# A one-core decoder step: the first weight block in two pieces, and gate products tied to the block three before

## The chip, the cores and the metric

The kernel runs on one core of a Trainium2 chip. The metric is the device time of one execution in microseconds (us), lower is better. Five engines work side by side on a core, each through its own queue in order: TensorE (PE, matrix products; PEld is its loading of weights), VectorE (DVE), ScalarE (ACT), GpSimd (POOL) and SyncE (SP, which here issues nearly all DMA transfers). They meet only at semaphores.

## The reference, cut to what matters

```python
# 512 prompt rows and 64 sample rows share the weights; D_MODEL = 1024
xn = rms_norm(x, attn_norm_g)
q, k, v, su, sv, g_a, g_b = split(xn @ w_in)             # 30 blocks of 128 columns
A  = window_attention(q, k, v)                           # window 128, 8 query heads
B  = gelu(su) * (W_s @ layer_norm(gelu(sv)))
x1 = x + (sigmoid(g_a) * (A @ w_branch_a) + sigmoid(g_b) * (B @ w_branch_b)) @ w_out
# product-key retrieval over 128 x 128 experts, 8 heads, 16 picks each
idx, gate = top16(rms_norm(x1) @ w_q, sub_keys)
x2 = x1 + sum_k gate_k * gelu(rms_norm(x1) . peer_u[idx_k]) * peer_v[idx_k]
x3 = x2 + sigmoid(rms_norm(x2) @ w_ple_gate) * (p @ w_ple)
```

All of it is in float32.

## The kernel before, in words

Every float32 matrix product is made of three products of split operands: a weight block `w_raw` is split into `w_hi` (a copy on ScalarE, line 66) and `w_lo` (what is left, a subtraction on VectorE, line 67), and so is the other operand. `load_block` allots `w_raw` (four buffers), issues its load on SyncE, and splits it with a raised priority. A scheduler sets the order of each engine's instructions when the kernel is built, from the order of the code, priorities, buffers and its own idea of durations; the order is fixed from then on.

**The start.** SyncE loads `vecs`, the first weight block (128 partitions x 8 x 128, 512 KB) and the eight tiles of the transposed input `xT[k]` (288 KB each; their buffers are called `c` or `c4` in the rows). ScalarE and VectorE split the weight block, scale and split each `xT[k]` into `xn[0][k]` and `xn[1][k]` (lines 181 and 182; tiles `x`), and sum the squares for the norm (squares line 140, sums line 142, tiles `rstd` and `t`). TensorE's first column chunk (`w_chunk(0)`, line 205) goes through k = 0 to 7 with six matmuls each (three products, two column ranges of 256 and 320), so that it can follow the input tiles as they come. Chunk 1 (tile `pv`, line 82) follows with the next weight block.

**The experts.** 384 of the rows are computed against all 16384 experts, in 128 blocks of 128. Stage 1 multiplies the rows by a block of `peer_u` (24 matmuls of 128x384, tiles `mm`) and keeps the activations. Stage 2 (from about 880 us; the loop over `j` of the diff) takes block j's activations, multiplies them by the gate weights `gsl` on VectorE (the gate product, line 987), splits the result into `wh` (ScalarE) and `wl` (VectorE, line 67), and multiplies by block j of `peer_v` (18 matmuls of 128x512 into `oacc`, line 951). In the loop's first part, up to j of about 85, each round also carries one block of stage 1, so TensorE has both kinds of work; after it stage 2 alone. `j1` counts the stage 1 blocks issued, `NJ` is 128. Up to 40 activations wait in memory (tiles `x4` and `aL`); those of even j from 2 to 38 (`SPILL`) were put out to DRAM and come back as `x1c`. The gate weights come from DRAM in 16 groups of eight blocks (`gs<-gd`, line 979, 1536 KB each) into two buffers in turn, so group g can be loaded only when the last product of group g-2 is done.

**The gathers.** The other 192 rows are computed by gathering expert rows one at a time: POOL issues an indirect DMA (line 721, 512 KB, five `row` buffers), and VectorE takes the row's dot product (`peer_u`, line 733) or adds it, weighted, to `acc` (`peer_v`, line 740). The function `pay` hands out gathers per block, 2.0 for a round of stage 2 alone. `after(ins, earlier)` is a dependency without a semaphore: it only tells the scheduler that one instruction has to stand behind another.

Of the kernel before, what the change touches and what calls it, by code (L numbers as in the profile page):

```python
# [7 lines left out]
F32 = mybir.dt.float32  # L8
F32R = mybir.dt.float32r
# [3 lines left out]
ALU = mybir.AluOpType  # L13
# [4 lines left out]
P = 128  # L18
# [3 lines left out]
KC = 8  # L22
NS = 64
NJ = 128
TB = 16
JB = 8
# [21 lines left out]
def tile_decoder_step(ctx: ExitStack, tc: tile.TileContext, a, o):  # L48
    nc = tc.nc
    V, A, T, G, S = nc.vector, nc.scalar, nc.tensor, nc.gpsimd, nc.sync  # L50

    def pool(stack, name, bufs, side="left", **kw):
        return stack.enter_context(tc.tile_pool(name=name, bufs=bufs, side=side, reuse_waits="tile", **kw))

    const = pool(ctx, "const", 1)
    wp = pool(ctx, "wp", 2)
# [3 lines left out]
    def cload(name, shape, pl=None):  # L60
        t = (pl or const).tile(shape, F32, name="c_" + name, bufs=1)
        S.dma_start(t, a[name])
        return t

    def split(src, hi, lo):
        A.activation(hi, src, AF.Copy)  # L66
        V.tensor_sub(lo, src, hi.bitcast(F32))  # L67

    def load_block(src, shape=(P, KC, P), urgent=True):
        raw = wp.tile(list(shape), F32, name="w_raw", bufs=4)  # L70
        S.dma_start(raw, src)
        hi = wp.tile(list(shape), F32R, name="w_hi", bufs=3)
        lo = wp.tile(list(shape), F32R, name="w_lo", bufs=3)
        with tc.high_priority(offset=1000 if urgent else 0):
            split(raw, hi, lo)
        return hi, lo
# [11 lines left out]
    def after(ins, earlier):  # L88
        tc.add_manual_dep(ins.ins, earlier.ins.name, mybir.DependencyInfo(
            mybir.DependencyClass.NoSync, mybir.DependencyReason.DATA), reason="pace")  # L90
# [28 lines left out]
    def f8(mk, *args):  # L119
        t = [mk(*args), mk(*args)]  # L120
        return [t[k // 4][:, k % 4, :] for k in range(KC)]
# [46 lines left out]

    vecs = cload("vecs", [P, 18])
    xT = f8(f4)  # L170
    first = [load_block(a["w_in"][0])]
    for k in range(KC):
        S.dma_start(xT[k], a["xT"][k])
    first.append(load_block(a["w_in"][1]))
    ident = cload("ident", [P, P])
    first.append(load_block(a["w_in"][2], urgent=False))
# [272 lines left out]
    def ple(tiles):  # L449
        wl_ = [load_block(a["w_ple"][k], (P, D)) for k in range(2)]  # L450
        for c0, r in tiles:
            pt = e1.tile([P, 2, P], F32, name="pw", bufs=3)
            S.dma_start(pt[:, :, :r], a["pT"][:, :, c0:c0 + r])
            ph, pl = (e1.tile([P, 2, P], F32R, name="pw", bufs=3) for _ in range(2))
            split(pt[:, :, :r], ph[:, :, :r], pl[:, :, :r])
            for hh in range(2):
                ps = bank("pv")
                i = 0
                for k in range(2):
                    for xi, wi in ((ph, 0), (ph, 1), (pl, 0)):  # L460
                        T.matmul(ps[:r], lhsT=xi[:, k, :r], rhs=wl_[k][wi][:, hh * 512:(hh + 1) * 512],  # L461
                                 start=i == 0, stop=i == 5)
                        i += 1
                st = e1.tile([P, 512], F32, name="st")
                A.activation(st[:r], ps[:r], AF.Copy)
                S.dma_start(pld[c0:c0 + r, hh * 512:(hh + 1) * 512], st[:r])
# [22 lines left out]
    for g in range(4):  # L489
        split(qT[:, g, :], ah[:, g, :], al[:, g, :])  # L490
# [222 lines left out]
    def gather(n, after):  # L713
        mark[0] = after
        for _ in range(n if steps else 0):
            next(steps[0], None)
            done[0] += 1
# [46 lines left out]
    def pay(x):  # L764
        credit[0] += x
        n = int(credit[0])
        credit[0] -= n
        gather(n, mark_pe[0])

    j1 = 0  # L770
# [5 lines left out]
    def stage1():  # L776
        nonlocal j1, nlive
        j = j1
        j1 += 1
        w = load_block(a["peer_uT"][j])  # L780
        ps = (mm() if j % 2 or phase[0] > 1 else bank("pv"))[:, :NB]
        tform(ps, w, xb)
        if j in SPILL:
            act = held_x[-1][:, sorted(SPILL).index(j) % 6, :]
        else:
            n = nlive % RING
            nlive += 1
            act = held_x[n // 6][:, n % 6, :] if n < NXP - 6 else (
                acp[0][:, n - NXP + 6, :] if n < RING - 6 else held_x[-1][:, n - RING + 6, :])
        A.activation(act, ps, AF.Gelu_apprx_tanh)  # L790
        acts[j] = act
        if j in SPILL:
            S.dma_start(ad[sorted(SPILL).index(j)], act)
        pay(GP[phase[0]])
# [15 lines left out]
    op = pool(gs_s, "op", 2)  # L810
# [77 lines left out]
    def add_x1(c):  # L888
        x1c = d3.tile([P, NB], F32, name="x1c")
        S.dma_start(x1c, x1d[c])  # L890
        for t in range(3):
            T.matmul(oacc[t][c // 4][:, (c % 4) * P:(c % 4 + 1) * P], lhsT=x1c[:, t * P:(t + 1) * P], rhs=ident,
                     start=False, stop=False)
# [32 lines left out]
    def gathered(ti):  # L926
        r = tilesA[ti][1]
        if r == NS:
            x2 = gp.tile([P, D], F32, name="xr")
            for hh in range(2):  # L930
                ps = mm()
                T.matmul(ps[:r], lhsT=ident2, rhs=accs[ti][:, hh * 512:(hh + 1) * 512], start=True, stop=True)
                A.activation(x2[:r, hh * 512:(hh + 1) * 512], ps[:r], AF.Copy)
        else:
            x2 = accs[ti]
        xn3 = spp[0].tile([P, D], F32, name="xn3")
        ss = gp.tile([P, 1], F32, name="ss")
        A.activation(xn3[:r], x2[:r], AF.Square, accum_out=ss[:r])
        tail_stat(ss, r)
        tail_scale(x2, ss, r, xn3)  # L940
        xhl = spp[0].tile([P, 2, KC, P], F32R, name="xhl")
        tail_turn(xn3, r, xhl[:, 0], xhl[:, 1])
        return x2, xhl[:, 0], xhl[:, 1], xn3, r, TILES[ti][0]
# [3 lines left out]
    def stage2(t, j, wh, wl, vh, vl):  # L947
        ts = slice(t * P, (t + 1) * P)
        for wi, vi, last in ((wh, vh, 0), (wh, vl, 0), (wl, vh, 1)):
            for hh in range(2):  # L950
                mark_pe[0] = T.matmul(oacc[t][hh], lhsT=wi[:, ts], rhs=vi[:, hh * 512:(hh + 1) * 512],  # L951
                                      start=j == 0 and last == 0 and vi is vh, stop=j == NJ - 1 and last == 1)

    tails, spp, back = [], [], {}
    for j in range(NJ):
        for jb in (2, 4) if j == 0 else (j + 4,):
            if jb in SPILL:
                back[jb] = d3.tile([P, NB], F32, name="x1c")
                S.dma_start(back[jb], ad[sorted(SPILL).index(jb)])
        if j and j - 1 not in SPILL and j1 < NJ:  # L960
            stage1()
        pay(G2[0] if j1 < NJ else G2[1])
        if j == TAIL0:
            aLs.close()
            xds.close()
            spp.append(pool(sps, "spare", 2, "right"))
            gather(max(0, P - done[0]), mark_pe[0])
            pg = gp.tile([P, D], F32, name="xr")
            S.dma_start(pg, a["ple_g"])
            tails.append(gathered(0))  # L970
        if j == TAIL1:
            gather(1000, mark_pe[0])
        if j == NJ - 2:
            tails.append(gathered(1))
        if j % JB == 0:
            gsl = gsp[(j // JB + 1) % 2].tile([P, NB // TB, JB, TB], F32, name="gs")
            nb = NB // TB if j else NB // TB - 1
            with tc.high_priority(offset=0 if j else 300):
                S.dma_start(gsl[:, :nb], gd[j // JB][:, :nb])
            if j == 0:  # L980
                A.activation(gsl[:, nb], g0, AF.Copy)
        vw = load_block(pv_view[j], (P, D))
        wf = acts.pop(j)
        if j in SPILL:
            wf = back.pop(j)
        wfv = wf.rearrange("p (b t) -> p b t", t=TB)
        V.tensor_tensor(wfv, wfv, gsl[:, :, j % JB, :], op=ALU.mult)
        wh = d2.tile([P, NB], F32R, name="wh")
        wl = d2.tile([P, NB], F32R, name="wl")
        split(wf, wh, wl)  # L990
        held.append((j, wh, wl, *vw))
        if j != NJ - 2:
            for t in range(3):
                for hj in held:
                    stage2(t, *hj)
            held.clear()
        if max(SPILL) < j <= max(SPILL) + KC:
            add_x1(j - max(SPILL) - 1)
# [150 lines left out]
```

## Time and profile before

| | us |
|---|---|
| median of 3 runs | 1764.59 (1763.62 to 1765.42) |
| the profiled execution, its own time | 1767.91 |
| its span in the trace | 1766.1 |
| TensorE busy in it | 1741.2 |
| VectorE busy | 1436.6 |
| ScalarE busy | 868.3 |

TensorE is busy for 99% of the span, so the time can fall only by what TensorE waits, or by what it does slowly; VectorE, at 81%, feeds it. A row's first number is the start in us from the start of the span, the second the duration.

### The profile page before, as it was taken

The numbers are of one execution on the slowest core, as the hardware profiler recorded it, in microseconds if no ns is written. First come the engines' busy times: TensorE is split into PE (matmuls) and PEld (weight loads), VectorE is DVE, ScalarE is ACT, GpSimd is POOL, SyncE is SP. The second block draws the span as 40 slices with busy tenths as digits, with TensorE's granted clock in tenths as the row PEclk, the third lists the DMA queues.
The fourth block names the chain that finished last, engine by engine and source line by source line (L and its number), as shares of the span: only waits on it lengthen the run. The fifth ranks groups of instructions, "written<-read, shape, count | busy, mean of one in ns | idle before, by whom it ended". The sixth has DMA issues, their size and how long they took to land.

```text
span 1766.1 us, 27818 instructions
## 1 busy us (share of the span) xinstructions
PE 1741.2 (99%) x10118; PEld 1574.5 (89%) x10118; DVE 1436.6 (81%) x2878; ACT 868.3 (49%) x1526; POOL 518.3 (29%) x390
## 2 busy tenths in 40 slices
PE   8999999999999899999999999999999999999999
PEld 8987999999999899999988888899999899887777
DVE  6355556549899999999898899998888888999963
ACT  6567443344335698998833333333333333333441
POOL 0000000000002112455245454454544544566300
PEclk9999999999999999999999999999999999999999
DMA  7211224443227577999999999999999999999832
GB/s 238 93 49 48 72 93 135 142 151 97 81 92 235 170 245 238 361 350 349 345 397 359 374 393 405 395 410 361 364 333 365 361 340 325 340 375 375 289 127 78
DMA packets 176601, 457.07 MB, mean 259 GB/s; under 512 B 15568, under 2 KB 77008, under 8 KB 174416
## 3 DMA queue, kind: packets, MB, share of 16 engines
q1 hardware_dynamic: 120880, 253.22, 40.9%
q0 software_dynamic: 55584, 202.07, 30.8%
q8 instruction: 79, 1.29, 0.3%
q14 instruction: 58, 0.48, 0.1%
HBM read 420.18 MB, written 35.78 MB: 258 GB/s over the span
## 4 chain that ended last, share of the span: by engine, by line
PE 81%; issue 6%; DVE 5%; DMA 4%; POOL 3%; ACT 1%; SPq 0%; POOLq 0%; DVEq 0%; ACTq 0%
PE mm L82 36%; PE oacc L951 24%; PE pv L82 5%; POOL row L721 3%; PE oacc L916 2%; PE sc L836 2%; PE pt L836 2%; DMA row<-peer_u,idx 2%; DMA row<-peer_v,idx 2%; PE sc L82 1%; DVE w_lo L67 1%; PE sc L594 1%; PE pv L461 1%; PE mm L916 1%; PE pv L329 1%
## 5 line engine op out<-in xcount | busy, mean ns | idle before, releaser
L66 ACT ACTIVATE w_hi<-w_raw 128x1024 fp32r<-128x1024 f32 x325 | 344.0, 1059 | 367.9 <-PE mm L82 265.5
L721 POOL DMA_INDIRECT row<-peer_u,idx x192 | 260.2, 1355 | 861.6 <-issue 515.2
L67 DVE TENSOR_TENSOR w_lo<-w_raw,w_hi 128x1024 fp32r<-128x1024 f32 x325 | 396.6, 1221 | 80.1 <-ACT w_hi L66 77.2
L82 PE MATMUL mm<-xd,w_hi 128*128 128x384 f32 x1552 | 405.7, 340 | 0.5 <-ACT w_hi L66 0.5
L721 POOL DMA_INDIRECT row<-peer_v,idx x192 | 256.6, 1337 | 240.5 <-DVE acc L740 215.2
L82 PE MATMUL mm<-x,w_hi 128*128 128x320 f32 (+1 forms) x1504 | 305.4, 297 | 0.0
L82 PEld LDWEIGHTS mm<-xd,w_hi 128*128 128x128 f32 x1552 | 281.3, 189 | 6.0 <-ACT w_hi L66 0.8
L82 PE MATMUL mm<-xd,w_lo 128*128 128x384 f32 x776 | 263.8, 340 | 1.6 <-DVE w_lo L67 1.6
L82 PEld LDWEIGHTS mm<-x,w_hi 128*128 128x128 f32 x1504 | 239.3, 188 | 12.5 <-issue 9.0
L740 DVE SCALAR_TENSOR_TENSOR acc<-row,wts,acc 128x1024 f32<-128x1024 f32 x192 | 245.7, 1279 | 2.1 <-DMA row<-peer_v,idx 1.6
L951 PE MATMUL oacc<-w_hi,wl 128*128 128x512 f32 x768 | 241.5, 396 | 2.3 <-DVE wl L67 2.3
L951 PE MATMUL oacc<-w_hi,wh 128*128 128x512 f32 x768 | 242.0, 395 | 1.3 <-ACT wh L66 1.3
L733 DVE SCALAR_TENSOR_TENSOR row<-row,xr 128x1024 f32<-128x1024 f32 x192 | 231.5, 1219 | 12.5 <-DMA row<-peer_u,idx 12.4
L951 PE MATMUL oacc<-w_lo,wh 128*128 128x512 f32 x768 | 241.5, 395 | 0.0
L82 PE MATMUL mm<-x,w_lo 128*128 128x320 f32 (+1 forms) x752 | 220.6, 294 | 0.0
L951 PEld LDWEIGHTS oacc<-w_hi,wl 128*128 128x128 f32 x768 | 144.1, 188 | 37.7 <-DVE wl L67 3.1
L951 PEld LDWEIGHTS oacc<-w_lo,wh 128*128 128x128 f32 x768 | 144.3, 188 | 34.5
L951 PEld LDWEIGHTS oacc<-w_hi,wh 128*128 128x128 f32 x768 | 143.5, 188 | 31.0 <-ACT wh L66 1.6
L82 PEld LDWEIGHTS mm<-xd,w_lo 128*128 128x128 f32 x776 | 146.7, 189 | 2.3 <-DVE w_lo L67 2.2
L82 PEld LDWEIGHTS mm<-x,w_lo 128*128 128x128 f32 x752 | 141.1, 188 | 1.1 <-issue 0.8
L82 PE MATMUL pv<-xd,w_hi 128*128 128x384 f32 x496 | 136.5, 347 | 0.7 <-ACT x L790 0.7
L66 ACT ACTIVATE wh<-x 128x384 fp32r<-128x384 f32 x66 | 34.7, 526 | 162.0 <-PE oacc L951 152.7
(326 smaller groups left out, 2383.4 us busy)
## 6 DMA issues: line engine op xcount, KB each, us to landing
w_raw<-peer_uT SPq DMA_DIRECT2D x128, 512.0 KB
w_raw<-peer_v SPq DMA_DIRECT2D x128, 512.0 KB
gd<-gs SPq DMA_DIRECT2D x24, 1024.0 KB
gs<-gd SPq DMA_DIRECT2D x15, 1536.0 KB
w_raw<-w_in SPq DMA_DIRECT2D x30, 512.0 KB
w_raw<-peer_wq SPq DMA_DIRECT2D x16, 512.0 KB
w_raw<-w_br SPq DMA_DIRECT2D x8, 512.0 KB
w_raw<-w_out SPq DMA_DIRECT2D x8, 512.0 KB
```

What stands on the lines that cost most here:

```text
L66: A.activation(hi, src, AF.Copy)
L67: V.tensor_sub(lo, src, hi.bitcast(F32))
L82: mark_pe[0] = T.matmul(ps, lhsT=w[wi][:, wk + k, :], rhs=x[xi][k], start=i == 0, stop=i == n - 1)
L329: T.matmul(pvs[pr, :], lhsT=vt[:, t0 + j, pr], rhs=pT, start=j == 0, stop=j == nk // P - 1)
L461: T.matmul(ps[:r], lhsT=xi[:, k, :r], rhs=wl_[k][wi][:, hh * 512:(hh + 1) * 512], start=i == 0, stop=i == 5)
L594: T.matmul(ps[:, b * P:(b + 1) * P], lhsT=qp[:, b * P:(b + 1) * P], rhs=sk, start=True, stop=True)
L721: ins = G.indirect_dma_start(out=row_, out_offset=None, in_=table, in_offset=bass.IndirectOffsetOnAxis(ap=ix, axis=0))
L733: V.scalar_tensor_tensor(row_, row_, 1.0, xrs[ti], op0=ALU.mult, op1=ALU.mult, accum_out=dots[:, s:s + 1])
L740: V.scalar_tensor_tensor(accs[ti], row_, wts[:, s:s + 1], accs[ti], op0=ALU.mult, op1=ALU.add)
L836: T.matmul(pt[:, t * P:(t + 1) * P], lhsT=oa[:, t, :], rhs=ob[:, t, :], start=True, stop=True)
L916: T.matmul(p[:r, :hs.stop - hs.start], lhsT=xi[:, k, :r], rhs=w[k][wi][:, hs], start=k == 0 and xi is xh and wi == 0, stop=k == KC - 1 and ...
L951: mark_pe[0] = T.matmul(oacc[t][hh], lhsT=wi[:, ts], rhs=vi[:, hh * 512:(hh + 1) * 512], start=j == 0 and last == 0 and vi is vh, stop=j = ...
```

## The change

The first weight block is loaded by hand instead of by `load_block`: k = 0 and 1 in a first transfer ahead of `xT[0]`, k = 2 to 7 in a second one behind `xT[0]`. Each piece is split on its own, with a priority of 1800 (1000 before). In stage 2 the gate product of block j, for j over 2 and as long as stage 1 blocks are left, has to stand on VectorE behind the subtraction that makes `wl` of block j-3; `split` returns that instruction for the purpose, and `lows` keeps it.

```diff
     def split(src, hi, lo):
         A.activation(hi, src, AF.Copy)
-        V.tensor_sub(lo, src, hi.bitcast(F32))
+        return V.tensor_sub(lo, src, hi.bitcast(F32))
...
     vecs = cload("vecs", [P, 18])
     xT = f8(f4)
-    first = [load_block(a["w_in"][0])]
+    wr0 = wp.tile([P, KC, P], F32, name="w_raw", bufs=4)
+    wr0s = [wp.tile([P, KC, P], F32R, name=nm, bufs=3) for nm in ("w_hi", "w_lo")]
+    first = [tuple(wr0s)]
+    cuts0 = (slice(0, 2), slice(2, KC))
+    S.dma_start(wr0[:, cuts0[0]], a["w_in"][0][:, cuts0[0]])
     for k in range(KC):
         S.dma_start(xT[k], a["xT"][k])
+        if k == 0:
+            S.dma_start(wr0[:, cuts0[1]], a["w_in"][0][:, cuts0[1]])
+    for q in cuts0:
+        with tc.high_priority(offset=1800):
+            split(wr0[:, q], *(w_[:, q] for w_ in wr0s))
     first.append(load_block(a["w_in"][1]))
...
-    tails, spp, back = [], [], {}
+    tails, spp, back, lows = [], [], {}, []
...
-        V.tensor_tensor(wfv, wfv, gsl[:, :, j % JB, :], op=ALU.mult)
+        gated = V.tensor_tensor(wfv, wfv, gsl[:, :, j % JB, :], op=ALU.mult)
+        if j > 2 and j1 < NJ:
+            after(gated, lows[j - 3])
         wh = d2.tile([P, NB], F32R, name="wh")
         wl = d2.tile([P, NB], F32R, name="wl")
-        split(wf, wh, wl)
+        lows.append(split(wf, wh, wl))
```

The scheduler moves instructions on several engines. VectorE at the start of the program, before (`w_lo` of the first block, then the low halves of the eight input tiles, then sums of squares and `w_lo` of the second block):

```order
L67 TENSOR_TENSOR w_lo<-w_raw,w_hi 128x1024
L182 SCALAR_TENSOR_TENSOR x_124<-c_92,c_vecs,x_122 128x576 x4
L182 SCALAR_TENSOR_TENSOR x_125<-c_93,c_vecs,x_123 128x576 x4
L142 TENSOR_TENSOR rstd<-rstd,t 128x576
L67 TENSOR_TENSOR w_lo<-w_raw,w_hi 128x1024
```

The same place now:

```order
L67 TENSOR_TENSOR w_lo<-w_raw,w_hi 128x256
L191 SCALAR_TENSOR_TENSOR x_127<-c_92,c_vecs,x_125 128x576
L67 TENSOR_TENSOR w_lo<-w_raw,w_hi 128x768
L191 SCALAR_TENSOR_TENSOR x_127<-c_92,c_vecs,x_125 128x576 x3
L191 SCALAR_TENSOR_TENSOR x_128<-c_93,c_vecs,x_126 128x576
L142 TENSOR_TENSOR rstd<-rstd,t 128x576
L191 SCALAR_TENSOR_TENSOR x_128<-c_93,c_vecs,x_126 128x576 x2
L142 TENSOR_TENSOR rstd<-rstd,t 128x576
L191 SCALAR_TENSOR_TENSOR x_128<-c_93,c_vecs,x_126 128x576
L142 TENSOR_TENSOR rstd<-rstd,t 128x576
L67 TENSOR_TENSOR w_lo<-w_raw,w_hi 128x1024
```

The first piece of `w_lo` and the first input tile stand alone at the head; two sums of squares more stand ahead of the second block's `w_lo`, and on ScalarE likewise two squares more ahead of its `w_hi`.

VectorE in stage 2 behind the `wl` of the thirtieth block, before (`x1c`, `aL` and `x` are activations that take a gate product, `row` is a gathered row):

```order
L67 TENSOR_TENSOR wl<-x_5599,wh 128x384
L987 TENSOR_TENSOR x1c<-x1c,gs 128x384
L987 TENSOR_TENSOR aL<-aL,gs 128x384 x4
L67 TENSOR_TENSOR w_lo<-w_raw,w_hi 128x1024
L733 SCALAR_TENSOR_TENSOR row,dots<-row,xr 128x1024
L67 TENSOR_TENSOR wl<-x1c,wh 128x384
```

The same place now:

```order
L67 TENSOR_TENSOR wl<-x_5602,wh 128x384
L996 TENSOR_TENSOR x_5602<-x_5602,gs 128x384
L996 TENSOR_TENSOR x1c<-x1c,gs 128x384
L67 TENSOR_TENSOR w_lo<-w_raw,w_hi 128x1024
L742 SCALAR_TENSOR_TENSOR row,dots<-row,xr 128x1024
L67 TENSOR_TENSOR wl<-x1c,wh 128x384
```

The run of four products for blocks far ahead is gone; one product for a block soon due stands there. Counted down the rows, the products before stand 11 blocks ahead of `wl` here, 40 ahead from the 44th block to the 88th; now they stand 1 or 2 ahead up to the 70th, 5 ahead at the 76th and 27 at the 88th.

VectorE in the late part of stage 2, where no stage 1 is left, before (numbers tell the blocks: `w_lo_16119` and `wl_16124` belong to one block, `w_lo_16154` and `wl_16159` to the next):

```order
L67 TENSOR_TENSOR w_lo_16119<-w_raw_16116,w_hi_16118 128x1024
L740 SCALAR_TENSOR_TENSOR acc_3945<-row_16008,wts_11141,acc_3945 128x1024
L67 TENSOR_TENSOR wl_16124<-x4_5597,wh_16123 128x384
L740 SCALAR_TENSOR_TENSOR acc_3945<-row_16040,wts_11141,acc_3945 128x1024
L67 TENSOR_TENSOR w_lo_16154<-w_raw_16151,w_hi_16153 128x1024
L740 SCALAR_TENSOR_TENSOR acc_3945<-row_16043,wts_11141,acc_3945 128x1024
L67 TENSOR_TENSOR wl_16159<-x4_5597,wh_16158 128x384
```

The same place now (`wl_16057` and `w_lo_16052` belong to one block, `w_lo_16087` and `wl_16092` to the next):

```order
L67 TENSOR_TENSOR w_lo_16052<-w_raw_16049,w_hi_16051 128x1024
L749 SCALAR_TENSOR_TENSOR acc_3948<-row_15939,wts_11144,acc_3948 128x1024
L996 TENSOR_TENSOR x4_5601<-x4_5601,gs_16294 128x384
L749 SCALAR_TENSOR_TENSOR acc_3948<-row_15971,wts_11144,acc_3948 128x1024
L67 TENSOR_TENSOR w_lo_16087<-w_raw_16084,w_hi_16086 128x1024
L749 SCALAR_TENSOR_TENSOR acc_3948<-row_15974,wts_11144,acc_3948 128x1024
L67 TENSOR_TENSOR wl_16057<-x4_5603,wh_16056 128x384
L749 SCALAR_TENSOR_TENSOR acc_3948<-row_16008,wts_11144,acc_3948 128x1024
L67 TENSOR_TENSOR w_lo_16122<-w_raw_16119,w_hi_16121 128x1024
```

Gate products now stand in this part too, 13 behind the 88th block, and for some 18 blocks a block's `wl` stands behind the next block's `w_lo` instead of ahead of it. On SyncE the loads of the gate groups go with the products: one per eight blocks up to the 78th load of `peer_v`, then four more up to the 91st.

## Rows read from the trace of the kernel before

**Rows 1.** Waits of TensorE: waiter, released by, us in total, times, longest.
```profile
PE mm L205 <- ACT x L181: 6.6, 1, 6.6
...
PE oacc L951 <- DVE wl L67: 2.3, 2, 1.6
...
PE mm L903 <- DVE xn L910: 0.9, 1, 0.9
```
**Rows 2.** Stretches: length; busy us of PE, PEld, DVE, ACT, POOL; clock; DMA; GB/s.
```profile
1100.00:1150.00 50.00, 47.74 (x235) 41.41 (x234) 46.42 (x75) 16.39 (x23) 23.18 (x18) 1.00 1.01 397
1430.00:1520.00 90.00, 90.00 (x455) 81.46 (x455) 78.50 (x78) 32.40 (x44) 46.67 (x36) 1.00 0.94 330
1520.00:1640.00 120.00, 119.96 (x510) 95.05 (x508) 115.56 (x115) 46.65 (x62) 79.22 (x56) 1.00 0.99 367
1640.00:1680.00 40.00, 39.13 (x173) 31.66 (x174) 35.37 (x38) 15.50 (x23) 12.09 (x10) 1.00 0.74 266
```
**Rows 3.** Timeline at 1127 us: start, us, instruction, [idle before it <-releaser].
```profile
1126.93 1.23 DVE L733 SCALAR_TENSOR_TENSOR row<-row,xr 128x1024 f32<-128x1024 f32 x1 [0.81 <-DMA row<-peer_u,idx]
...
1128.56 1.49 DVE L987 TENSOR_TENSOR x<-x,gs 128x384 f32<-128x384 f32 x3
1128.69 0.73 PE L951 MATMUL oacc<-w_hi,wl 128*128 128x512 f32 x2 [1.63 <-DVE wl L67]
```
**Rows 4.** Timeline of SyncE, first and last of seven gate loads.
```profile
1062.18 0.33 SPq L979 DMA_DIRECT2D gs<-gd  x1
...
1185.45 0.33 SPq L979 DMA_DIRECT2D gs<-gd  x1
```
**Rows 5.** Timeline of ScalarE at the start.
```profile
4.79 1.06 ACT L66 ACTIVATE w_hi<-w_raw 128x1024 fp32r<-128x1024 f32 x1 [2.76 <-DMA w_raw<-w_in]
5.75 1.61 ACT L181 ACTIVATE x<-c,c_vecs 128x576 fp32r<-128x576 f32 x2
7.94 3.74 ACT L181 ACTIVATE x<-c,c_vecs 128x576 fp32r<-128x576 f32 x5 [0.59 <-DMA c<-xT]
...
12.83 0.67 ACT L140 ACTIVATE t<-c 128x576 f32<-128x576 f32 x1
13.40 1.04 ACT L66 ACTIVATE w_hi<-w_raw 128x1024 fp32r<-128x1024 f32 x1
```
**Rows 6.** Timeline of VectorE at the start.
```profile
5.87 1.23 DVE L67 TENSOR_TENSOR w_lo<-w_raw,w_hi 128x1024 fp32r<-128x1024 f32 x1 [4.80 <-ACT w_hi L66]
7.01 1.54 DVE L182 SCALAR_TENSOR_TENSOR x<-c,c_vecs,x 128x576 fp32r<-128x576 f32 x2
...
13.69 0.75 DVE L142 TENSOR_TENSOR rstd<-rstd,t 128x576 f32<-128x576 f32 x1
14.48 1.23 DVE L67 TENSOR_TENSOR w_lo<-w_raw,w_hi 128x1024 fp32r<-128x1024 f32 x1
```
**Rows 7.** Timeline of TensorE at the start.
```profile
9.44 0.41 PE L205 MATMUL mm<-x,w_lo 128*128 128x256 f32 x1
...
10.88 0.41 PE L205 MATMUL mm<-x,w_lo 128*128 128x256 f32 x1
...
16.86 0.28 PE L82 MATMUL pv<-x,w_lo 128*128 128x256 f32 x1
```
**Rows 8.** Timeline of one round of the late part of stage 2.
```profile
1563.74 0.53 ACT L66 ACTIVATE wh<-aL 128x384 fp32r<-128x384 f32 x1 [2.67 <-PE oacc L951]
...
1564.21 1.07 ACT L66 ACTIVATE w_hi<-w_raw 128x1024 fp32r<-128x1024 f32 x1
1564.30 0.56 DVE L67 TENSOR_TENSOR wl<-aL,wh 128x384 fp32r<-128x384 f32 x1
...
1564.77 1.28 DVE L740 SCALAR_TENSOR_TENSOR acc<-row,wts,acc 128x1024 f32<-128x1024 f32 x1
...
1565.97 1.22 DVE L67 TENSOR_TENSOR w_lo<-w_raw,w_hi 128x1024 fp32r<-128x1024 f32 x1
...
1568.50 0.56 DVE L67 TENSOR_TENSOR wl<-aL,wh 128x384 fp32r<-128x384 f32 x1
```

## The prediction, made before the changed kernel ran

> **What bounds the kernel now.** I read the busy times first: TensorE works 1741.2 of 1766.1 us, so an edit can only pay where TensorE stands still, or where it runs at its lower clock. So the waits of TensorE come next [rows 1]. Of the waits in reach of this change, 6.6 us is one piece at the very start, for the first scaled input tile; 2.3 us is two waits of the retrieval products for `wl`; and 0.9 us is the wait for a normalised row tile late in stage 2. Then I read the timeline around each, to see which engine is late and what stands in front of it there. Everything in reach adds up to less than 10 us, and most of the 6.6 is the first loads themselves, so the change is worth a few us at most. The profiled execution took 1767.91 us, 3.3 above the median of 1764.59; I work out shifts in the profiled one and apply them to the median.
>
> **The start.** Before, ScalarE begins with `w_hi` at 4.79 us, when the whole first block has landed, needs 1.06 for it, and scales the first input tile from 5.75 [rows 5]; TensorE's first product begins at 6.56, the length of its wait [rows 1]; the first low half stands on VectorE behind the whole `w_lo`, from 7.01, half of 1.54 [rows 6]. After, the first piece of the weights (128 KB) and the first input tile (288 KB) make 416 KB, less than the 512 KB that had landed by 4.79; so the tile is there a little earlier, I take 4.5. The quarter of `w_hi` (some 0.3) is done by then. Scaling takes 0.8 (half of 1.61), so the first product begins at 5.3 to 5.6, 1.0 to 1.3 sooner, and the first low half is done at about 6.2 instead of 7.8.
>
> Little of that gets through. Behind tile 0 now stand the other three quarters of the split (0.8 on ScalarE, 0.9 on VectorE) ahead of tile 1, whose low half I see done at about 8.4. TensorE would be past the second k step at about 9.4 where it was at 10.45: a lead of 1.05 us. A k step lasts 1.44 us there [rows 7]: 1728 columns, which is 1.2 GHz, the lower of the two levels. At 16.86 the same product takes 0.28 that takes 0.41 here [rows 7], so the upper level comes between; if the rise comes at the same moment as before, the lead is worth 0.5 us from then on; if it comes as much sooner as the work does, 1.05. And then comes the second weight block. Before, it is split at once: `w_hi` at 13.40, `w_lo` at 14.48, done at 15.71, and TensorE comes to the first product with it at 16.86 [rows 5 to 7]. Now ScalarE has two squares more ahead of `w_hi` (0.67 each) and VectorE two sums more ahead of `w_lo` (0.75 each), so `w_lo` is done at 16.7 to 17.2: 15.71 and 1.4 to 1.5, less what the earlier input tiles give back at one end. TensorE would come there, with two more `w_hi` products moved ahead of it (640 columns, 0.27 at the upper level), at 17.13 less its lead, 16.1 to 16.6. So it waits, and of the lead 0 to 0.4 us is left. I take **-0.3**. The bounds are -1.3 (nothing on the way eats the lead) and +0.3 (the second block is late by more than the lead).
>
> At this place the rows price no split transfer: the first block comes as one load, with 4 KB per partition. The Trainium skill says in "Perfetto Trace Analysis", section "DMA Optimizations", that transfers under 2 KB carry a significant overhead for each one, and in its next point that splitting may let some work start sooner; the first piece here has 1 KB per partition. No run here shows which of the two wins; by the first point the start would give 0 instead of -0.3 and the time 0.3 more.
>
> **The burst that goes.** Before, the gate products run ahead from 11 blocks to 40 between about 1060 and 1200 us, and each group finished frees a buffer, so that seven gate loads of 1536 KB lie between 1062 and 1185 us [rows 4]. In that stretch the queues move 397 GB/s [rows 2]. At 1127 a gathered row comes 0.81 us late on VectorE, three gate products (1.49 us, 0.50 each) stand behind it, `wl` behind these, and TensorE waits 1.63 for `wl` [rows 3]; the other wait of the 2.3 is of the same kind [rows 1]. In the changed order no product stands there that is not soon due, and the loads come one per eight blocks. So **-2.2** us goes. That is the safest term: it has two causes, the burst of loads and the run of products, and the change takes away both.
>
> **The burst that comes back.** The tie ends with the stage 1 blocks. The products' lead grows from 5 blocks at the 76th to 27 at the 88th, and four gate loads follow each other between the 82nd and the 91st load of `peer_v`, about 85 us at 1430 to 1520. There the queues move 330 GB/s now [rows 2]; four loads of 1.57 MB in 85 us add 74, so about 404 GB/s, as at 1100. The rows gathered there are needed in the same way. The price lies between 0 and the 2.2 paid at 1100; VectorE, with 11.5 us idle in 90 against 3.6 in 50 [rows 2], is the less loaded here, but four loads come where it was seven. I take half: **+1.1**.
>
> **The late part.** 35 products, 17.5 us of VectorE work, move from before 1430 to after it. VectorE's idle time there is 11.5 up to 1520, 4.4 up to 1640 and 4.6 up to 1680 [rows 2], 20.5 in all. 22 products (11.0 us) fall into the first stretch, nearly its whole idle time; 13 (6.5 us) come behind it against 9.0. It fits, but barely, and idle time is not always where a product stands. What is queued behind a product is the dot products of gathered rows and the splits. In a round of stage 2 alone (4.20 us from one `wl` to the next [rows 8]) `wl` now stands behind the next block's `w_lo` for some 18 blocks. The chain is then: `wh` 0.47 to the start of `w_hi`, `w_hi` 1.06, `w_lo` 1.14, one gathered row 1.20, `wl` 0.55, by the distances and durations of [rows 8], 4.4 us. TensorE needs `wl` one round after the buffer is freed, and 4 of 18 products into it: 4.20 + 0.9 = 5.1. So the slack falls from 5.1 less the 1.1 that `wh` and `wl` take now to 0.7: no wait, as long as no product (0.50) and no late row (0.8 at 1127) fall into one round together. If they do in some rounds, TensorE waits some tenths in each. Bounds 0 and +4 (18 blocks of about 0.2); I take **+0.4**, near the lower end, as most of these rounds carry no product. The 0.9 at the normalised tile stays: its transposes stand a little later on TensorE, but the tile comes later on VectorE too.
>
> **The rest** costs nothing: `split` returning an instruction issues nothing, the tie has no semaphore, and from 120 to 870 us the orders are the same on every engine. The number of loads is one more.
>
> **Sum**: -0.3 - 2.2 + 1.1 + 0.4 = -1.0, so 1764.59 - 1.0 = **1763.6**.
>
> **Rivals.** (A) Everything in reach goes: the start gives its full 1.3, the 2.2 go without a new burst, and the 0.9 at the normalised tile goes as the loads there are spread differently: -4.4, 1760.2. For it: POOL and VectorE have some idle time in 1430 to 1520. Against it: the second weight block is later by the order, and the four loads stand in the order too. (B) Slower: VectorE becomes the bound of late stage 2. It decides from the point where a round's chain is longer than 5.1 us, that is, where a product or a late row of over 0.7 us falls between a `w_lo` and the `wl` behind it; VectorE is busy 115.56 of 120 us in 1520 to 1640 [rows 2], so what is late there is not caught up. Then 18 blocks lose 0.25 to 0.3 us, about 5, with the new burst 1.1, less 2.5: +3.7, 1768.3. For it speaks how full VectorE is; against it that only 13 products fall there and that the gathered rows, which could wait, can be put off. (C) The burst only changes its place: the same 2.2 is paid at 1430 to 1520, and the rest cancels: -0.3 to +0.1, 1764.4. It would mean that the tie ends too early to do what it says.
>
> **How the numbers follow.** About 0.2%, 3.5 us, is what a measurement of this kernel can tell from no change. My forecast has 0.4, C 0.25, A 0.18, and B 0.17. A reaches the line of 1761.06 in nearly all of its cases, and a better start than I take adds some of the forecast's: 0.2 for faster. B crosses 1768.12 in most of its cases: 0.17 for slower; 0.63 is left for no change. The range from 1760.2 to 1768.3 goes from A to B and leaves out about half of each, some 2 in 10.
>
> **What would show it.** At the start: `w_hi` in two pieces, the first product at 5.3 to 5.6, then a new wait of TensorE for the second block's `w_lo` at 16 to 17 us. The waits of the retrieval products for `wl` gone from 1060 to 1200, the rate there at 340 to 370 instead of 397; a rate of about 400 at 1430 to 1520, with waits for `wl` behind late rows of up to 2.2. From 1520 on, VectorE at 97% or more, and no wait of more than some tenths a round. The forecast is wrong if the wait for the first tile falls below 5.0 us and no later wait takes its place (A), or if waits for `wl` appear in round after round behind `w_lo` (B).

## The result, and the profile after

| | before | changed |
|---|---|---|
| median, us | 1765.74 (1763.62 to 1767.34) | 1776.51 (1774.72 to 1779.78) |
| the profiled execution, its own time | 1767.91 | 1774.72 |
| TensorE busy in it | 1741.2 | 1743.6 |

The change makes the kernel slower: the ratio is 1.006, 95% interval 1.0047 to 1.0072, some 8 to 13 us. The prediction was 1763.6 with a range up to 1768.3; the time lies above it. The profiled execution of the changed kernel is the fastest of its six and that of before is slower than any of its six, so the two traces differ by 6.8 us where the medians differ by 10.8.

The waits of TensorE after (columns as in [rows 1]):

```profile
PE oacc L960 <- DVE wl L67: 7.7, 5, 3.3
PE mm L214 <- ACT x L190: 6.1, 1, 6.1
```

The wait for `wl` was to vanish. It grew from 2.3 to 7.7 us. Where, shows a comparison of the n-th matmul of both traces (start in us, and the difference):

```
n      before    after    after - before
60       18.04     18.21     +0.17
5940    891.68    891.48     -0.20
7080   1132.65   1129.66     -2.99
9120   1537.41   1535.88     -1.53
9180   1551.41   1552.24     +0.83
9240   1565.41   1571.22     +5.81
9600   1650.46   1657.36     +6.90
```

The start gives nothing, and the old burst between 892 and 1133 us gives back 2.8 us, where 2.2 were forecast. From there to 1565 us 8.8 us are lost, 7.3 of them in 28 us of the program, between 1537 and 1565 us of the kernel before. Stretches of the changed kernel (columns as in [rows 2], whose 1430 to 1520 answers the second line; the third is the place of the loss):

```profile
1060.00:1200.00 140.00, 140.00 (x707) 124.44 (x706) 117.46 (x176) 47.74 (x64) 65.58 (x52) 1.00 0.97 365
1430.00:1520.00 90.00, 90.00 (x450) 80.74 (x450) 82.37 (x94) 32.34 (x44) 49.70 (x34) 1.00 0.98 377
1520.00:1560.00 40.00, 34.13 (x136) 25.83 (x135) 37.05 (x39) 10.98 (x15) 24.99 (x18) 0.96 0.99 375
1560.00:1640.00 80.00, 80.00 (x339) 63.18 (x338) 77.91 (x80) 29.70 (x41) 53.66 (x38) 1.00 1.00 371
```

TensorE is busy 34.13 of 40 us at 1520 to 1560; before it was 40.00 of 40. VectorE is not full there either: 37.05 of 40. What it waits for is the key. Waits of VectorE from 1380 to 1640 us (waiter, released by, us, times, longest), changed kernel:

```profile
DVE acc L749 <- DMA row<-peer_v,idx: 5.4, 6, 1.6
DVE wl L67 <- ACT wh L66: 5.0, 6, 0.9
DVE w_lo L67 <- ACT w_hi L66: 2.6, 5, 0.9
DVE aL L996 <- DMA gs<-gd: 2.4, 1, 2.4
```

And the kernel before:

```profile
DVE w_lo L67 <- ACT w_hi L66: 10.9, 12, 0.9
DVE wl L67 <- ACT wh L66: 6.8, 17, 0.5
DVE acc L740 <- DMA row<-peer_v,idx: 1.3, 3, 0.5
```

Before, VectorE waited 17.7 us for ScalarE and 1.3 for transfers. A wait for ScalarE means that VectorE is early. Now it waits 7.8 us for transfers, 5.4 for gathered rows and 2.4 for a gate load, and only 7.6 for ScalarE. It runs late. The timeline of all engines in the round that costs most (start, us, instruction, [idle before <-releaser]; lines of SyncE, GpSimd and the other matmuls left out):

```profile
1540.54 1.29 DVE L749 SCALAR_TENSOR_TENSOR acc<-row,wts,acc 128x1024 f32<-128x1024 f32 x1 [1.55 <-DMA row<-peer_v,idx]
...
1551.97 0.53 ACT L66 ACTIVATE wh<-aL 128x384 fp32r<-128x384 f32 x1 [2.67 <-PE oacc L960]
1552.06 0.55 DVE L996 TENSOR_TENSOR x<-x,gs 128x384 f32<-128x384 f32 x1
...
1552.53 1.28 DVE L749 SCALAR_TENSOR_TENSOR acc<-row,wts,acc 128x1024 f32<-128x1024 f32 x1
...
1553.73 1.22 DVE L67 TENSOR_TENSOR w_lo<-w_raw,w_hi 128x1024 fp32r<-128x1024 f32 x1
...
1554.87 1.27 DVE L749 SCALAR_TENSOR_TENSOR acc<-row,wts,acc 128x1024 f32<-128x1024 f32 x1
1556.06 0.55 DVE L67 TENSOR_TENSOR wl<-aL,wh 128x384 fp32r<-128x384 f32 x1
...
1556.66 1.22 PE L960 MATMUL oacc<-w_hi,wl 128*128 128x512 f32 x2 [3.33 <-DVE wl L67]
```

`wh` is made at 1551.97, and `wl` could follow half a microsecond later. But a gate product, two gathered rows and the next block's `w_lo` stand ahead of it, and VectorE has had no gap since the row that came 1.55 us late at 1540.54. `wl` is done at 1556.61, and TensorE has stood 3.33 us. Behind the wait a pair of matmuls takes 1.22 us, where the pair behind a wait in [rows 3] takes 0.73: the granted clock is at its lower level for a while. The difference of the two traces grows by 4.98 us between the 9180th and the 9240th matmul, 3.33 of it the wait; the 1.65 that are left go to the clock. The stretch behind the wait, whose granted clock is 0.61:

```profile
1557.00:1560.50 3.50, 3.50 (x11) 2.71 (x11) 3.50 (x4) 0.00 (x0) 2.19 (x3) 0.61 1.00 382
```

### The profile page after: what moved, and what is told of

The parts are those of the page before. It is cut to its first block, busy times and chain, and to the rows that moved or that the text cites. A ratio compares the mean times of both kernels' runs of the same rounds, so it can differ in the third digit from the quotient of the medians.

```text
span 1772.9 us, 27801 instructions
## 1 busy us (share of the span) xinstructions
PE 1743.6 (98%) x10118; PEld 1574.0 (89%) x10118; DVE 1435.1 (81%) x2879; ACT 867.3 (49%) x1527; POOL 524.4 (30%) x390
## 4 chain that ended last, share of the span: by engine, by line
PE 81%; issue 5%; DVE 5%; DMA 4%; POOL 3%; ACT 1%; SPq 0%; POOLq 0%; ACTq 0%; DVEq 0%
PE mm L82 36%; PE oacc L960 26%; PE pv L82 4%; POOL row L730 3%; DMA row<-peer_v,idx 2%; PE oacc L925 2%; PE sc L845 2%; PE sc L82 1%; PE pt L845 1%; DVE w_lo L67 1%; DMA row<-peer_u,idx 1%; PE sc L603 1%; PE pv L470 1%; PE mm L925 1%; PE pv L338 1%
## 5 line engine op out<-in xcount | busy, mean ns | idle before, releaser
L66 ACT ACTIVATE w_hi<-w_raw 128x1024 fp32r<-128x1024 f32 (+1 forms) x326 | 344.0, 1056 | 357.0 <-PE mm L82 268.1
L67 DVE TENSOR_TENSOR w_lo<-w_raw,w_hi 128x1024 fp32r<-128x1024 f32 (+1 forms) x326 | 397.0, 1219 | 70.8 <-ACT w_hi L66 67.8
L730 POOL DMA_INDIRECT row<-peer_v,idx x192 | 265.3, 1382 | 241.7 <-DVE acc L749 215.4
```

What stands on the lines that cost most here:

```text
L67: return V.tensor_sub(lo, src, hi.bitcast(F32))
L730: ins = G.indirect_dma_start(out=row_, out_offset=None, in_=table, in_offset=bass.IndirectOffsetOnAxis(ap=ix, axis=0))
```

## The experiments

Times below are medians; ratios are against the kernel before, run on the same chip in the same session, with 95% intervals. They are not the quotients of the medians and differ from them by up to 0.0009, 1.6 us, so differences of 1 to 2 us between runs say little. Lines of code carry the changed kernel's names.

**Which of the two parts.** First each alone.

> The kernel before with the new start alone; the gate products stand as before. Theory: the start moves nothing that lasts (TensorE's first product 0.5 us sooner, given back at the second block's w_lo by 18 us), and the whole loss comes from the tie. Expected: within 1.0 us of before, and the waits for wl at 1110 to 1130 as before, 2.3 us. Rival: the other start sets something for the whole program (the moments at which the clock rises, the phase of the loads) and carries part of the 10.8 us: then 3 to 10 us slower.

```diff
-        if j > 2 and j1 < NJ:
-            after(gated, lows[j - 3])
```

Measured: 1765.22 against 1765.15, ratio 0.9997 (0.9989 to 1.0006). The start is worth nothing that this can tell, within 1 to 2 us. The old waits for `wl` are there again, as expected:

```profile
PE oacc L960 <- DVE wl L67: 2.5, 2, 1.6
```

> The kernel before with the tie of the gate products alone; the start is that of before. Theory: the loss is all of the tie's: 9 to 12 us slower than before, with 7 to 9 us lost between 1520 and 1560 us and 2 to 3 gained between 1060 and 1140. Rival (the start carries part of it): 1 to 7 slower.

```diff
-    first = [tuple(wr0s)]
+    first = [load_block(a["w_in"][0])]
```

(and the two pieces with their loads and splits taken out). Measured: 1775.06 against 1765.15, ratio 1.0058 (1.0040 to 1.0075). The tie alone brings the loss, within the interval of 7 to 13 us.

**Is it the time of the products, their order, or the loads?** Three suspects stand at 1430 to 1560: more products on VectorE, `wl` behind the next `w_lo` (from 1556 us on in the changed kernel), and four gate loads in a row.

> The changed kernel with the tie kept for all blocks, also when no stage 1 block is left. So no run of products and no four gate loads in a row between the 82nd and the 91st block: one load in eight blocks or more. But some 40 products (20 us of VectorE) stand in the part where stage 2 is alone, against 35 from 1430 on in the changed kernel. Theory (VectorE has too little room once stage 1 has ended, and a wl that stands behind the next w_lo shows it): 8 to 20 us slower than the changed kernel, with waits for wl spread over 1520 to 1660. Rival (the four gate loads make the gathered rows late, and those rows are the cause): no burst, no late rows: 5 to 10 us faster than the changed kernel, about level with before.

```diff
-        if j > 2 and j1 < NJ:
+        if j > 2:
```

Measured: 1781.57, ratio 1.0089 (1.0072 to 1.0105), 5 us slower than the changed kernel. That is less than I gave for the theory, and far from the rival. The loss is elsewhere now: TensorE stands 5.14 us for `wl` at 1649.79, and 6.2 us for `wh` in six waits. With all products at the end, VectorE alone is enough for a loss, without a burst of loads. It does not tell what the changed kernel dies of.

> The changed kernel, with one more dependency without a semaphore: once stage 1 has ended, a block's w_lo has to stand behind the block before's wl, as it stands in the kernel before. Products, gate loads and gathered rows stay where the change put them. Theory (wl behind the next w_lo takes the slack, some 3.5 us a round, and this is what turns a late VectorE into a wait of TensorE): 5 to 9 us faster than the changed kernel. Rival (VectorE lacks time as such, whatever the order): within 2 us of the changed kernel, TensorE then waiting for w_lo instead of wl.

```diff
-        with tc.high_priority(offset=1000 if urgent else 0):
-            split(raw, hi, lo)
+        with tc.high_priority(offset=1000 if urgent else 0):
+            low = split(raw, hi, lo)
+            if behind is not None:
+                after(low, behind)
...
-        vw = load_block(pv_view[j], (P, D))
+        vw = load_block(pv_view[j], (P, D), behind=lows[-1] if j1 == NJ and lows else None)
```

Measured: 1770.97, ratio 1.0031 (1.0017 to 1.0046): 5.8 us above before, so half of the loss comes back, 5 us, the lower end of what the theory gave. The waits for `wl` are still there, but short. The longest one in the late part:

```profile
1553.80 0.73 PE L962 MATMUL oacc<-w_hi,wl 128*128 128x512 f32 x2 [0.98 <-DVE wl L67]
```

The three waits that stand ahead of the first block with the new order stay much as they were (0.94, 0.66 and 0.45 here, 0.93, 0.67 and 0.94 in the changed kernel); the long one behind them falls from 3.33 to 0.98. So the order makes a late VectorE dear, but does not make it late.

**The loads.** Two kernels take one suspect away, one puts the bare traffic back, and two shift the rows or the burst.

> The changed kernel without the last four gate loads (groups 12 to 15; the products of blocks 96 to 127 take the gates of group 11, which is another computation). Products, order and inversions as in the changed kernel (24 blocks with wl behind the next w_lo); only the transfers and the wait for them are gone. Rival (the loads make VectorE late: 2.41 us for a gate load at 1486, 5.4 us for rows): 6 to 10 us faster than the changed kernel. Theory (the products' own time and the order are the larger part): 2 to 4 us faster than the changed kernel, since the 2.41 us of VectorE's wait come back, and part of the late rows.

```diff
-        if j % JB == 0:
+        if j % JB == 0 and j // JB < 12:
             gsl = gsp[(j // JB + 1) % 2].tile([P, NB // TB, JB, TB], F32, name="gs")
```

Measured: 1767.07 against 1765.57, ratio 1.0011 (1.0000 to 1.0021): 9.3 us of the 10.8 are gone, and not the 2 to 4 of the theory, although all products and the 24 inversions of `wl` and `w_lo` are as they were. VectorE has never been so full in that stretch, and TensorE does not wait in it:

```profile
1430.00:1520.00 90.00, 90.00 (x451) 80.86 (x450) 87.80 (x104) 32.55 (x44) 58.40 (x36) 1.00 0.94 344
```

My first theory, that the products' own time and the order are the larger part, fell here. What is left are two waits for `wl`, 1.00 us at 1550.30 and 1.78 at 1645.30. The second stands in the changed kernel too (1653.05), and not in e4.

> The changed kernel with the gate products of the last 35 blocks (j over 92) done for one element in sixteen only (24 of 384 columns), so that each takes VectorE some 0.1 instead of 0.5 us, 14 us less in all; the rest of these activations stays unweighted, which is another computation. The gate loads stay where they are. The scheduler then sets wl behind the next w_lo in 6 blocks, not in 24. Theory (the moved products fill VectorE): the loss goes: 8 to 12 us faster than the changed kernel. Rival (the loads): 0 to 4 us faster than the changed kernel.

```diff
-        gated = V.tensor_tensor(wfv, wfv, gsl[:, :, j % JB, :], op=ALU.mult)
+        tn = 1 if j > 92 else TB
+        gated = V.tensor_tensor(wfv[:, :, :tn], wfv[:, :, :tn], gsl[:, :, j % JB, :tn], op=ALU.mult)
```

Measured: 1767.08, ratio 1.0011 (1.0001 to 1.0020). Taking most of the products' time away, with the loads left, also brings 9.3 us back. But this kernel changes the order as well: in the late part `wl` stands where it stood before the change. E4, with that order and the full products, still loses 5.8 us, so of the 9.3 some 4 are the products' time and the rest can be the order's. VectorE waits for the loads more than before (waits from 1380 to 1640):

```profile
DVE x L997 <- DMA gs<-gd: 6.6, 3, 3.2
```

and can mostly bear it; the one wait of TensorE in that stretch, 2.26 us at 1504.11 for `w_lo`, stands behind the longest of these. So e7 is the products with their order, e8 the loads, and each alone leaves a kernel 1.5 us slower than before. That is a net figure: every trace of a kernel with the tie has the 2.8 us that the old burst gives back. With these added the late part costs 4.3 us in e7, 4.3 in e8 (each to within 2 us) and 13.6 in the changed kernel, 5 more than the two together. In the traces alone, from the 7080th matmul to the 9600th, it is 2.4 and 3.7 against 9.9. What the two share is VectorE's idle time; the balance below tries that.

> The kernel of e7_no_late_gate_loads with the four gate loads put back as traffic only: they are issued near the 83rd to the 89th load of peer_v, as in the changed kernel, into a buffer that no product reads (the products of blocks 96 to 127 still take the gates of group 11, which is another computation). So no product waits for a load, but the queues carry them. E7 took 1.5 us more than before, the changed kernel 10.8 more. Theory (the traffic makes gathered rows late on VectorE): 6 to 11 us slower than before. Rival (the wait of a product for its gate load, 2.41 us on VectorE at 1486, with all that stands behind it): within 2.5 us of before.

```diff
+            late = j // JB > 11
-            gsl = gsp[(j // JB + 1) % 2].tile([P, NB // TB, JB, TB], F32, name="gs")
+            gsn = gsp[1 if late else (j // JB + 1) % 2].tile([P, NB // TB, JB, TB], F32, name="gs")
...
+            if late:
+                after(gload, pvl[{12: 83, 13: 84, 14: 87, 15: 92}[j // JB]])
+            else:
+                gsl = gsn
```

(`pvl` holds the loads of 128x1024 blocks; products read `gsl`, loads go to `gsn`.) Measured: 1774.92 against 1765.61, ratio 1.0049 (1.0035 to 1.0062). No late product waits for these loads, and yet the loss is 9.3 us again, 7.8 more than in e7. The traffic does it, and what comes late on VectorE are the gathered rows: 7.0 us against 2.0 in e7. Weight blocks come late too, which they do not in the changed kernel: ScalarE waits 11.0 us for them between 1497 and 1513 us. TensorE is busy for all of 1430 to 1520 here, so these waits cost nothing at once; whether they add to what VectorE lacks afterwards is not shown. Waits of VectorE from 1200 to 1640, and TensorE's:

```profile
DVE acc L752 <- DMA row<-peer_v,idx: 7.0, 6, 2.4
```

```profile
PE oacc L963 <- DVE wl L67: 8.4, 4, 3.5
```

> The changed kernel with the gathers paid out otherwise: 1.8 a round while stage 1 lasts (1.6 before) and 1.6 a round after it (2.0 before). Some 17 gathered rows, each 1.28 us on VectorE, move out of the late part; the tie and the products stay, and the scheduler then sets wl behind the next w_lo in 6 blocks, not in 24. Theory (VectorE has no room in the late part): the waits for wl from 1520 to 1560 go, 6 to 11 us faster than the changed kernel. Rival (the gate loads between 1465 and 1521 make rows and products late, whatever VectorE's room): within 3 us of the changed kernel, the waits only moved to earlier.

```diff
-G2 = (1.6, 2.0)
+G2 = (1.8, 1.6)
```

Measured: 1777.22, ratio 1.0071 (1.0058 to 1.0084): a miss. I had moved rows off the full late part, but into the very burst, where rows are late: VectorE waits 10.9 us for rows instead of 5.4, and TensorE stands up to 4.58 us at 1542.87. The new order is left in 6 blocks only, and the longest wait stands at one of them. Fewer rows in a round don't help when those in the burst come later.

> The changed kernel with the tie ended at block 60 instead of with the stage 1 blocks, so that the products run ahead and the gate loads follow each other between the 58th and the 67th load of peer_v, at 1240 to 1330 us, where stage 1 still runs and VectorE is busy 83 to 88% of the time. Theory (what the burst costs is set by what VectorE has to spare behind it: late rows and gate waits of 5 to 8 us are caught up there, and no product is left for the late part): within 2.5 us of before, waits for wl of 0 to 3 us. Rival (a burst costs the same wherever it stands): 7 to 11 us slower than before.

```diff
-        if j > 2 and j1 < NJ:
+        if 2 < j < 60:
```

Measured: 1767.16 against 1765.61, ratio 1.0000 (0.9991 to 1.0009). The same kind of burst, five gate loads between 1262 and 1327 us, where VectorE is less full (85.51 of 100 us at 1200 to 1300 in the kernel before), costs no more than the one of before: 1.0 us in the trace, lost between 1334 and 1360 us. No wait for `wl` stands among TensorE's seven longest. VectorE waits there too, from 1200 to 1640:

```profile
DVE acc L749 <- DMA row<-peer_v,idx: 4.2, 10, 0.8
DVE row L742 <- DMA row<-peer_u,idx: 3.1, 6, 1.1
DVE x L996 <- DMA gs<-gd: 2.9, 1, 2.9
```

That is 10.2 us of waits for transfers with next to no loss behind them. The changed kernel has 9.5 in the same stretch and loses 9.9. In the kernel before, the old burst (1060 to 1200 us) made rows later than the new one does, and cost 2.8:

```profile
DVE row L733 <- DMA row<-peer_u,idx: 7.5, 12, 1.5
```

So the lateness of the rows by itself does not set the price.

The balance of VectorE from 1430 to 1560 us puts these runs in one row each. Before, VectorE is idle 130 - 78.50 - 38.74 = 12.8 us there and spends 6.1 us on gate products. Each run's products above 6.1 and its waits for transfers have to fit into the 12.8:

```
                 products above  waits for  sum   TensorE stands
                 those of before transfers        1430 to 1560, us
changed               11.6          7.8     19.4      5.9
e2 (tie alone)        11.0          8.3     19.3      6.1
e9 (traffic)          12.6          7.0     19.6      6.6
e6 (rows earlier)     11.4         12.6     24.0      9.6
e4 (wl ahead)         11.6          8.3     19.9      3.3
e7 (no loads)         12.6          2.0     14.6      1.0
e8 (no products)       4.6          9.6     14.2      2.3
e3 (tie to the end)    3.7          0.0      3.7      1.6
e5 (ramp)              1.1          0.4      1.5      0.0
e11 (early burst)      0.4          1.1      1.5      0.0
```

(The products come from the busy time of their line in that stretch, for the changed kernel 15.13 + 2.59 - 6.07; the waits from VectorE's timeline.) What TensorE stands goes with the sum, except in e3, whose 1.6 us are a wait for ScalarE's `wh` and whose loss comes behind this stretch. It is a rough balance, since a wait can fall into time that was idle anyway; e7 and e8, a little over 12.8, show that it need not cost more than 1 to 2 us there. With `wl` ahead (e4) the same overrun costs half. That the waits come about by the sum, and not by one late transfer at a bad place, is argued from these rows; no run changes the idle time alone.

**A version that beats both.** If neither the products nor the loads come in a heap, both the old and the new burst should go.

> The changed kernel with another tie: the product of block j stands behind wl of a block whose distance grows evenly, from 3 at the 20th block to 43 at the last, for all blocks (17 + (j - 20) * 67 // 107, and j - 3 where that is smaller). So the products end before the 85th block as in the kernel before, but no gate loads follow each other faster than one in 4 to 6 blocks, and no product stands in the late part. Theory (the loss is VectorE work moved into the full late part, the gain the burst at 1060 to 1200 that goes): the loss goes whole and the gain stays: 1.5 to 3.5 us faster than before, no wait for wl over 1 us. Rival (the tie itself, by the order that it makes, costs something in 900 to 1400): within 1 us of before or slower.

```diff
-        if j > 2 and j1 < NJ:
-            after(gated, lows[j - 3])
+        if j > 2:
+            after(gated, lows[min(j - 3, 17 + (j - 20) * 67 // 107)])
```

Measured: 1764.23 against 1765.57, ratio 0.9989 (0.9980 to 0.9998). There is no wait for `wl` or `wh` among TensorE's seven longest, and the old burst's stretch runs through:

```profile
1060.00:1200.00 140.00, 140.00 (x707) 124.46 (x706) 122.94 (x189) 47.73 (x64) 66.82 (x52) 1.00 0.99 380
```

> The kernel before with the evenly growing tie of e5_ramp, and the start of before. Theory (the start is worth nothing in either direction, the tie's 1.3 us come from the burst that goes): 1 to 3.5 us faster than before, like e5_ramp within 1 us. Rival (the start gives something that e5 shows): slower than e5_ramp by over 1 us.

The same tie with the start of before. Measured: 1763.66 against 1765.61, ratio 0.9985 (0.9976 to 0.9995), 1 to 4 us faster than before and some 13 faster than the changed kernel. The two starts don't differ by more than these runs can tell.

## Why the prediction was wrong, step by step

**The start: forecast -0.3, measured 0.** The mechanism was right, a lead that is lost at the second block. Lines of the changed kernel's start (start, us, instruction):

```profile
4.41 0.42 ACT L66 ACTIVATE w_hi<-w_raw 128x256 fp32r<-128x256 f32 x1 [2.38 <-DMA w_raw<-w_in]
...
5.23 0.77 ACT L190 ACTIVATE x<-c,c_vecs 128x576 fp32r<-128x576 f32 x1 [0.40 <-DMA c<-xT]
...
10.55 0.28 PE L214 MATMUL mm<-x,w_lo 128*128 128x256 f32 x1
...
15.89 1.22 DVE L67 TENSOR_TENSOR w_lo<-w_raw,w_hi 128x1024 fp32r<-128x1024 f32 x1
...
17.16 0.38 PE L82 MATMUL pv<-x,w_lo 128*128 128x256 f32 x1 [0.48 <-DVE w_lo L67]
```

The first tile came at 5.23, not 4.5, so the first product began at 6.06 instead of 5.3 to 5.6. TensorE ran at the upper level by 10.55 (a product of 256 columns takes 0.28, as at 16.86 in [rows 7]); before, the same form still took 0.41 at 10.88. That early rise belongs to this execution and not to the start: in e1, with the same start and a first product at 5.68, the form takes 0.28 only from 13.32 on, and before from 13.69. Even with it nothing is left: the second block's `w_lo` is done at 17.11, inside the forecast 16.7 to 17.2, and TensorE's first product with it begins at 17.16 where the old pace gave 17.13. The Trainium skill's two points on small transfers ("Perfetto Trace Analysis", section "DMA Optimizations") are not told apart by the time: e1's interval holds both 0 and -0.3. The rows lean to the second: the first piece releases `w_hi` at 4.41 (3.67 in e1) where the whole block did at 4.79, and the 0.50 us that the first product gains are lost at `w_lo`.

**The burst that goes: forecast -2.2, measured -2.8** between the 5940th and the 7080th matmul. The rate at 1060 to 1200 is 365 GB/s, inside the 340 to 370 that I named. E5 and e10 keep this gain. This step held.

**The burst that comes back and the late part: forecast +1.1 and +0.4, measured +9.9** from the 7080th to the 9600th matmul in the traces. This is the step that failed. I had its parts: 22 products or 11.0 us into 11.5 idle (9.6 measured up to 1520, 11.6 up to 1560), four loads that bring the rate up (377 measured at 1430 to 1520, against my 404), late rows, `wl` behind `w_lo` with 0.7 us of slack. The four loads came within 55 us, from 1465.84 to 1521.16, and not within 85. But I priced the loads as if VectorE still had its idle time, and the products as if rows came in time. Both were paid out of the same idle time. The range for the loads came from the burst at 1100, 2.2 us. There VectorE can catch up behind it; from 1520 on, by [rows 2], it is 96% busy, and in the terms of the sum I used that row only for the products; only rival B has it for what comes late. E7 and e8 show the two terms apart: the products with their order cost some 4.3 us (2.4 in the trace) where I had 0.4, the loads some 4.3 (3.7 in the trace) where I had 1.1. So each was sized too low by itself, and together they cost some 5 us more (3.8 in the traces) than their sum. E11 shows that a burst with room behind it costs no more than the old one did.

**Rival B** had the place (late stage 2), the condition (a late row or a product between a `w_lo` and the `wl` behind it) and the chain of events right, and 0.17 of the chance. Its price of 3.7 was too low for two reasons: I spread the loss evenly as 0.25 to 0.3 us over 18 blocks (24 have the new order), while it comes as few long waits (five of 7.7 us in all) when the lateness of several rows has piled up; and I left out that TensorE's clock can fall behind a long wait, another 1.65 us in this trace.

**Rivals A and C** fell: the start gave nothing, and the burst did not merely move: the late part cost several times the old price, 9.9 us against 2.8 in the traces.

**What stays open.** The traces account for 6.8 of 10.8 us. The other executions of the changed kernel have spans up to 1778.0 with a mean granted clock down to 0.994, against 1772.9 and 0.997 in the profiled one. A difference of 0.003 of the span is about 5 us, so more falls of the clock would account for it, but no trace of this kernel shows where they lie. E9's profiled execution, with a clock of 0.994, has such falls behind its waits of 3.53 and 1.78 us. Another part can lie ahead of stage 2. The orders agree there from 120 to 870 us, and still the traces differ, at the 5940th matmul from 2.9 us ahead of before's (e1) to 3.6 behind (e11).

## What to carry to other kernels

Two costs that each fit into an engine's idle time don't fit together: add up, for one stretch, the work moved in and the waits for transfers that it brings, and compare the sum with that engine's idle time there and in the stretch behind. When a tie ends, what it held back comes at once; look where that is, and let the tie loosen evenly instead. To tell a late engine from an early one read whom it waits for: VectorE's waits for ScalarE fell from 17.7 to 7.6 us, and those for transfers rose from 1.3 to 7.8.

## What was new about the hardware

Gathered rows came late behind bulk loads although the queues moved less than in the old burst (404 GB/s at 1060 to 1200): with four gate loads of 1536 KB issued between 1431 and 1498 us the rate at 1430 to 1520 went from 330 to 377 GB/s, and VectorE waited 5.4 us for rows. In e9, where no late product depends on these loads, it waited 7.0, in e7 without them 2.0.

A wait of TensorE is followed by its lower clock in some executions and not in others. Behind the 3.33 us in the changed kernel the granted clock was 0.61 from 1557.0 to 1560.5, 1.65 us more. Behind the same wait in e2 the pair of matmuls takes 0.73 and not 1.22:

```profile
1554.64 0.73 PE L951 MATMUL oacc<-w_hi,wl 128*128 128x512 f32 x2 [3.31 <-DVE wl L67]
```

And behind the wait of 1.78 us that both e9 and the changed kernel have, six matmuls take 2.64 us in e9 and 1.67 in the changed kernel:

```profile
1654.98 2.64 PE L963 MATMUL oacc<-w_hi,wl 128*128 128x512 f32 x6 [1.78 <-DVE wl L67]
1653.05 1.67 PE L960 MATMUL oacc<-w_hi,wl 128*128 128x512 f32 x6 [1.78 <-DVE wl L67]
```

In e4, with waits of 0.98 at most in that part, the granted clock of 1520 to 1560 stayed at 1.00. The rise at the start moves likewise from one execution to the next: with the same new start a product of 256 columns takes 0.28 from 10.55 us on in the changed kernel's trace and from 13.32 on in e1's.
